# Hybrid MLA and Mamba-2 trunk on one core: flat joint moving operand, SSM scores one step later, gated y transposed through both bank pairs

## Chip, cores and metric

The kernel runs on one core of one Trainium2 chip. The core has a matrix engine (TensorE, PE in the profile; its weight loads are PEld), a vector engine (DVE), a scalar engine (ACT), GpSimd (POOL), and a queue engine (SP) that issues most DMAs. The metric is the device time of one execution in microseconds. The kernel before took 2306.25 us (median of 3 runs, 2304.0 to 2308.58).

## What is computed

The reference is a trunk of two layers over 256 tokens with 2048 channels. Layer 0 mixes tokens with multi-head latent attention (MLA), layer 1 with a Mamba-2 state space block (SSM); each mixer is followed by a dense MLP with squared ReLU and 8192 hidden channels, and everything is pre-norm and residual. Cut to what the change touches:

```python
def ssm_mixer(h, w_in, conv_w, conv_b, dt_bias, a_log, d_skip, norm_g, w_out):
    z, xbc, dt = jnp.split(h @ w_in, ...)
    xbc = silu(causal_depthwise_conv(xbc, conv_w, conv_b))
    xs, b_in, c_in = jnp.split(xbc, ...)        # 8 groups; b_in, c_in have 128 states each
    cb = einsum('blgn,bsgn->blsg', c_c, b_c)    # the scores of a group
    y = einsum('blsgh,bsghp->blghp', cb * decay, x_c) + d_skip * xs
    y = y * silu(z)                             # gated y
    y = rms_norm over each group of 512 channels
    return y @ w_out

def squared_relu_mlp(h, w_in, w_out):
    u = relu(h @ w_in)
    return (u * u) @ w_out
```

The sequence is one chunk of 256, so there is no state carried between chunks.

## The kernel before, in words

**Products in three parts.** Every large product is made from split numbers. A weight tile (128 x 1024 f32, two k tiles of 512 columns) arrives by DMA as `wraw`. ACT copies it rounded into `wh` (line 102), and DVE subtracts to get the rest, `wl` (line 103). Activations are split in the same way. PE then does high times high, low times high and high times low into one PSUM bank. One such piece of weights is called a unit here; in a plain block it is twelve matmuls of 512 columns, eight with `wh` (lines 328 and 329) and then four with `wl` (line 332). There are four `wh` and four `wl` buffers, and the conversions run up to three units ahead.

**Activations as stationary or as moving operand.** The normalised activations lie in four `xt` tiles made by `pair()` (line 278): `[P, 2, 4, 256]`, that is first the high parts of four k tiles and then their low parts. In the plain blocks 128 x 128 pieces of them are the stationary operand. In `column_unit` (line 420) the weights are stationary and the activations move: the matmul of line 425 takes high and low of one k tile together as 2 x 256 moving columns, which lie 1024 elements apart, and that of line 427 takes the high 256 columns alone against `wl`. `column_unit` makes the first columns of each MLP (tiles `cf`) and b and c of the SSM (tiles `acc`).

**Ticks.** The order of PE's instructions is the order in which the program text emits them. Around the blocks, small pieces of work are put off with `self.later(n, fn)`, and `tick()`, called after each key of a block (24 matmuls, two units) and inside `bc_columns`, counts them down: `later(0, ...)` runs at the next tick, `later(2, ...)` at the third. The order on DVE, ACT, POOL and SP is made by a scheduler that sees data dependences and buffers; each engine then runs its list in order.

**SSM.** For each of the 8 groups, `bc_columns(g)` makes b and c, `conv` convolves them (lines 1131 to 1142, result `bc`, one buffer), and `cb_group(g)` makes the scores `cb` on PE (lines 1199 and 1200) into an `sm` bank, which DVE masks (line 1203) and ACT copies (line 1208). `x_block(g)` makes and convolves x and asks for the heads; `head` multiplies decay and scores into `mt` (line 1296), and when eight heads are there `products` runs 64 small matmuls (line 1311) into two `yp` banks, y_0 and y_1. `across` (line 1265) is the far half. `z_block(g)` makes the gate; `gate` multiplies it in, normalises, and `transposes` (line 306) turns the gated y with PE (line 313), after which ACT and DVE split it into k tiles (lines 302 and 303). The order of the steps is the list `SSM_ORDER`: b0, d0, x0, b1, x1, b2, x2, z0, b3, x3, z1, b4, x4, z2, o0 and so on.

**PSUM.** Eight banks: `acc` has four, `sm` two and `yp` two. `bank(wide)` (line 266) gives an `sm` bank when `wide` is False, and takes `yp` and `sm` in turn when it is True. The two transposes of a gated y (one for each half of the tokens) call it with False and take both `sm` banks.

Of the kernel before, what the change touches and what calls it, by code (L numbers as in the profile page):

```python
# [21 lines left out]
F32R = mybir.dt.float32r  # L22
# [6 lines left out]
P = 128  # L29
# [185 lines left out]
class Trunk:  # L215
# [60 lines left out]
        return pool.tile([P, 4, 256], dt, tag=pool.name, name=self.name(pool.name))  # L276

    def pair(self, dt=F32R):
        return self.xtp.tile([P, 2, 4, 256], dt, tag="xt", name=self.name("xt"))

    def rsqrt(self, ssq, n, width, eps=EPS, scale=None):
# [139 lines left out]
    def column_unit(self, acc, unit, xw, half):  # L421

        h, lo = (v.rearrange("p (k n) -> p k n", n=P) for v in unit)
        nc = self.nc
        high = lambda k: nc.tensor.matmul(acc.rearrange("p (i n) -> p i n", i=2), h[:, k], xw[2 * half + k // 4][:, :, k % 4],  # L425
                                          start=half == 0 and k == 0, stop=half == 1 and k == 7)
        low = lambda k: nc.tensor.matmul(acc[:, 0:256], lo[:, k], xw[2 * half + k // 4][:, 0, k % 4], start=False, stop=False)
        for k in range(8):
            for fn in ((low, high) if half and k == 7 else (high, low)):
                fn(k)  # L430
# [636 lines left out]
    def ssm_body(self, sp, dp, gain):  # L1067
        nc, d, cst = self.nc, self.d, self.cst
# [5 lines left out]
        dt = sp.tile([P, 2, 64], F32, name="dt")  # L1074
# [26 lines left out]
        def behind(what):  # L1101
            return self.tc.issue_after(getattr(self.flow, what).ins)
# [14 lines left out]
        def bc_columns(g):  # L1117
            accs = [self.acc_tile() for _ in range(2)]
            for half in range(2):
                for i in range(2):  # L1120
                    self.column_unit(accs[i], self.flow.next(("sb", i, g, half))[1], self.xT, half)
                    if i == 0:
                        self.tick()
            s, a, th = (self.scratch() for _ in range(3))
            of = lambda v: v.rearrange("p (i n) -> p i n", i=2)
            for i in range(2):
                nc.scalar.activation(of(s)[:, i], accs[i][:, 256:512], AF.Copy)
                nc.vector.tensor_tensor(of(s)[:, i], accs[i][:, 0:256], of(s)[:, i], ALU.add)

            def conv():  # L1130
                nc.vector.tensor_tensor(of(s), of(s), row.unsqueeze(1).to_broadcast([P, 2, S]), ALU.mult)
                for i in range(2):
                    c = 8 * i + g
                    wc = lambda k: cst[:, C_CW + 4 * c + k:C_CW + 4 * c + k + 1]
                    u, o = of(s)[:, i], of(a)[:, i]
                    nc.scalar.activation(o, u, AF.Identity, bias=cst[:, C_CB + c:C_CB + c + 1], scale=wc(3))
                    for k in (2, 1, 0):
                        m = 3 - k
                        nc.vector.scalar_tensor_tensor(o[:, m:256], u[:, 0:256 - m], wc(k), o[:, m:256], ALU.mult, ALU.add)
                nc.scalar.activation(th, a, AF.Tanh, scale=0.5)  # L1140
                bc[g] = sp.tile([P, 2, S], F32, tag="bc", name=f"bc{g}", bufs=1)
                nc.vector.scalar_tensor_tensor(bc[g].rearrange("p i n -> p (i n)"), th, 1.0, a, ALU.add, ALU.mult)

            self.later(0, conv)
            self.later(2, lambda: cb_group(g))

        def dt_block():
            self.narrow_block(("si", "dt", 0, 0), self.xT, dt_chain)
# [47 lines left out]
        def cb_group(g):  # L1196
            B, C = bc[g][:, 0], bc[g][:, 1]
            b = self.bank(False)
            nc.tensor.matmul(b[:, 0:256], B[:, 0:P], C, start=True, stop=True)
            nc.tensor.matmul(b[:, 256:384], B[:, P:256], C[:, P:256], start=True, stop=True)  # L1200
            t = sp.tile([P, 384], F32, tag="cb", name=f"cb{g}", bufs=3)
            for o in (0, 256):
                nc.vector.scalar_tensor_tensor(t[:, o:o + P], b[:, o:o + P], 0.125, tri[:, 0:P], ALU.mult, ALU.mult)
            cb[g] = t

            def far_part():
                with behind("last"):
                    nc.scalar.activation(t[:, P:256], b[:, P:256], AF.Copy, scale=0.125)

            self.later(0, far_part)  # L1210
# [111 lines left out]
        yT = [None] * GROUPS  # L1322

        def z_block(g):
            accs = self.block([("si", "z", g, q) for q in range(4)], xT)
            ng = self.gain_tile(d["sng"][g])
            ssq = self.stat(2)
            ws = []
            for t in range(2):
                w = self.scratch()  # L1330
                nc.scalar.activation(w, accs[t], AF.Tanh, scale=rsh[t])
                nc.vector.scalar_tensor_tensor(w, w, 1.0, accs[t], ALU.add, ALU.mult)
                ws.append(w)
            yT[g] = (self.ktile(self.k4), self.ktile(self.k4))

            def gate():
                if g not in ready:
                    self.later(0, gate)
                    return
                for t in range(2):  # L1340
                    x = xg[g][t]
                    nc.gpsimd.tensor_tensor(x, ws[t], x, ALU.mult)
                    self.square_sum(x, ssq[:, t:t + 1], scale=rs[t])
                rr = self.rsqrt(ssq, 2, 512, 4 * EPS)
                r = self.stat(2)
                nc.vector.tensor_tensor(r, rr, rs2, ALU.mult)
                for t in range(2):
                    nc.vector.scalar_tensor_tensor(ws[t], xg[g][t], r[:, t:t + 1], ng, ALU.mult, ALU.mult)
                    self.later(1, lambda t=t: self.transposes(ws[t], yT[g][0], yT[g][1], t, False))
                self.later(1, lambda: gated.add(g))  # L1350

            self.later(1, gate)
# [6 lines left out]
        for step in SSM_ORDER:  # L1359
            kind, i = step[0], int(step[1])  # L1360
            if kind == "b":
                bc_columns(i)
            elif kind == "d":
                dt_block()
            elif kind == "x":
                x_block(i)
            elif kind == "z":
                z_block(i)
            elif i < 3:
                for nb in range(4) if len(step) == 2 else ((0, 1) if step[2] == "a" else (2, 3)):  # L1370
                    self.add_residual(nb, o_block(i, nb))
            else:
                self.boundary_begin(gain)
                for pair in ((0, 1), (2, 3)):
                    accs = {}
                    for nb in pair:
                        accs[nb] = self.block([("so", 6, nb)], self.from_tiles(yT[6:8]), last=False)
                    for nb in pair:
                        self.block([("so", 7, nb)], self.from_tiles(yT[7:8]), accs=accs[nb], first=False)
                        self.finalize(nb, accs[nb], False)  # L1380
                self.boundary_end()
# [228 lines left out]
```

## Time and profile before

| | us |
|---|---|
| median of 3 runs | 2306.25 |
| lowest and highest of them | 2304.0 and 2308.58 |
| the profiled execution, its own time | 2310.83 |
| span of that execution in the profile | 2309.0 |
| PE busy in the span | 2290.7 |
| DVE busy | 1930.3 |
| ACT busy | 1398.8 |
| POOL busy | 208.5 |

Rows of the timeline read: start in us, length in us, engine, line, operation, output and inputs, shape, how many instructions are merged, and in brackets the idle time just before, with what ended it. The ends of matmuls are modelled, since they are pipelined: a single 512-column matmul is shown as 0.39 us, though the next one starts 0.227 us after it. Starts are therefore the safer part of a row. The windows view gives for each stretch the busy time of each engine with its number of instructions, then the granted TensorE clock (1.00 is full speed), the DMA share and GB/s.

### The profile page before, as it was taken

What the parts mean: (1) busy time and instruction counts of PE and PEld (TensorE: products, weight loads), DVE (VectorE), ACT (ScalarE), POOL (GpSimd) and SP (SyncE); (2) the same over time, 40 slices, a digit from 0 to 9 for tenths busy, and PEclk for the clock granted to TensorE, in tenths of its full rate; (3) what the DMA queues carried; (4) which work ended last, traced back from release to release, by engine and by line L of the source; (5) the groups of instructions that cost most, each with busy time, mean ns of one, the idle gap of its engine ahead of it and who ended that gap; (6) DMA issues with size and microseconds to landing.
All of it is one profiled execution on the core that took longest, in us unless ns stands there. A gap on an engine that the chain in (4) does not pass through costs nothing.

```text
span 2309.0 us, 30976 instructions
## 1 busy us (share of the span) xinstructions
PE 2290.7 (99%) x11125; PEld 1908.9 (83%) x11125; DVE 1930.3 (84%) x2379; ACT 1398.8 (61%) x1997; POOL 208.5 (9%) x233
## 2 busy tenths in 40 slices
PE   9999999999999999999999999999999999999999
PEld 8888888888888888888778888888888888888887
DVE  7776798899899897769788678777989889889885
ACT  7775576566666656555555555545666656666663
POOL 1430000000000000002122012120000000000000
PEclk9999999999999999999999999999999999999999
DMA  8444677887887878678777776666688788787874
GB/s 315 147 133 150 206 223 253 260 238 250 262 243 247 268 210 268 196 226 315 259 235 234 248 242 223 223 204 197 201 250 239 251 264 249 239 268 240 250 230 163
DMA packets 161915, 538.02 MB, mean 233 GB/s; under 512 B 17680, under 2 KB 26832, under 8 KB 160736
## 3 DMA queue, kind: packets, MB, share of 16 engines
q1 hardware_dynamic: 151264, 502.36, 65.6%
q0 software_dynamic: 8096, 29.41, 7.8%
q10 hardware_dynamic: 2400, 4.27, 0.5%
q8 instruction: 87, 1.43, 0.3%
q14 instruction: 68, 0.56, 0.1%
HBM read 529.56 MB, written 6.41 MB: 232 GB/s over the span
## 4 chain that ended last, share of the span: by engine, by line
PE 84%; DVE 9%; DMA 3%; issue 2%; POOL 1%; ACT 1%; SPq 0%; DVEq 0%; ACTq 0%; POOLq 0%
PE acc L328 10%; PE acc L329 10%; PE acc L332 10%; PE yp L620 8%; PE yp L621 8%; PE yp L619 8%; PE st L620 7%; PE st L621 7%; PE st L619 7%; DVE wl L103 4%; PE sm L313 2%; PE acc L425 1%; DMA wraw<-mi 1%; DVE xtm L1243 1%; DVE wraw L183 1%
## 5 line engine op out<-in xcount | busy, mean ns | idle before, releaser
L102 ACT ACTIVATE wh<-wraw 128x1024 fp32r<-128x1024 f32 (+1 forms) x818 | 857.4, 1053 | 578.8 <-PE acc L329 247.7
L103 DVE TENSOR_TENSOR wl<-wraw,wh 128x1024 fp32r<-128x1024 f32 (+1 forms) x818 | 983.0, 1216 | 224.1 <-ACT wh L102 213.0
L619 PE MATMUL yp<-wh,k 128*128 128x512 f32 x896 | 350.1, 391 | 0.0
L620 PE MATMUL yp<-wl,k 128*128 128x512 f32 x896 | 349.0, 389 | 0.2 <-DVE wl L103 0.2
L621 PE MATMUL yp<-wh,k 128*128 128x512 f32 x896 | 349.0, 389 | 0.0
L102 ACT ACTIVATE wh<-wrx 128x1024 fp32r<-128x1024 f32 x168 | 177.7, 1059 | 126.2 <-PE yp L621 101.3
L103 DVE TENSOR_TENSOR wl<-wrx,wh 128x1024 fp32r<-128x1024 f32 x168 | 203.9, 1219 | 34.8 <-ACT wh L102 34.6
L328 PE MATMUL acc<-wh,xt 128*128 128x512 f32 x576 | 229.2, 398 | 0.4 <-ACT wh L102 0.4
L329 PE MATMUL acc<-wh,xt 128*128 128x512 f32 x576 | 225.2, 391 | 0.0
L620 PEld LDWEIGHTS yp<-wl,k 128*128 128x128 f32 x896 | 168.2, 188 | 35.4 <-DVE wl L103 0.9
L621 PEld LDWEIGHTS yp<-wh,k 128*128 128x128 f32 x896 | 168.2, 188 | 35.2
L619 PEld LDWEIGHTS yp<-wh,k 128*128 128x128 f32 x896 | 168.2, 188 | 34.7
L328 PE MATMUL acc<-wh,k 128*128 128x512 f32 x496 | 196.5, 396 | 0.0
L329 PE MATMUL acc<-wh,k 128*128 128x512 f32 x496 | 193.2, 390 | 0.0
L619 PE MATMUL st<-wh,xt 128*128 128x512 f32 x448 | 177.2, 396 | 0.0
L620 PE MATMUL st<-wl,xt 128*128 128x512 f32 x448 | 174.8, 390 | 0.0
L621 PE MATMUL st<-wh,xt 128*128 128x512 f32 x448 | 174.8, 390 | 0.0
L332 PE MATMUL acc<-wl,xt 128*128 128x512 f32 x576 | 154.3, 390 | 1.9 <-DVE wl L103 1.9
L199 POOL DMA_DIRECT2D wrx<-mi x56 | 49.1, 877 | 1142.2 <-DVE wl L103 977.1
L332 PE MATMUL acc<-wl,k 128*128 128x512 f32 x496 | 132.9, 390 | 0.7 <-DVE wl L103 0.7
L620 PE MATMUL st<-wl,sN 128*128 128x512 f32 x336 | 131.1, 390 | 1.7 <-DVE wl L103 1.7
L619 PE MATMUL st<-wh,sN 128*128 128x512 f32 x336 | 132.1, 393 | 0.0
(303 smaller groups left out, 3694.4 us busy)
## 6 DMA issues: line engine op xcount, KB each, us to landing
wraw<-mo SPq DMA_DIRECT2D x256, 512.0 KB, 5.3
wraw<-mi SPq DMA_DIRECT2D x224, 512.0 KB, 5.4
wraw<-si SPq DMA_DIRECT2D x128, 512.0 KB, 4.8
wraw<-so SPq DMA_DIRECT2D x64, 512.0 KB, 4.7
wrx<-mi SPq DMA_DIRECT2D x56, 512.0 KB, 4.8
wrx<-mi POOLq DMA_DIRECT2D x56, 512.0 KB, 8.0
wraw<-wo SPq DMA_DIRECT2D x32, 512.0 KB, 3.9
wraw<-mc SPq DMA_DIRECT2D x32, 512.0 KB, 4.4
```

The source lines that it names most:

```text
L102: self.last = nc.scalar.activation(h[:, v], raw[:, v], AF.Copy)
L103: self.last_lo = nc.vector.tensor_tensor(lo[:, v], raw[:, v], h[:, v].bitcast(F32), ALU.subtract)
L183: add = lambda out, a, b: nc.vector.tensor_tensor(st[out].tile, st[a].tile, st[b].tile, ALU.add)
L199: nc.gpsimd.dma_start(st["b11"].tile, quarter(d, 1, 0), accum_op=ALU.add)
L313: self.nc.tensor.transpose(b[:, j * P:(j + 1) * P], src[:, j * P:(j + 1) * P], self.ident)
L328: nc.tensor.matmul(accs[t][:, :n], ah, wh[:, q, :], start=first and kt + q == 0, stop=False)
L329: nc.tensor.matmul(accs[t][:, :n], al, wh[:, q, :], start=False, stop=False)
L332: nc.tensor.matmul(accs[t][:, :n], lhs(kt + q, t)[0], wl[:, q, :], start=False, stop=en and q == nk - 1)
L425: high = lambda k: nc.tensor.matmul(acc.rearrange("p (i n) -> p i n", i=2), h[:, k], xw[2 * half + k // 4][:, :, k % 4], start=half == 0 a ...
L619: nc.tensor.matmul(b, ah, wh, start=first and q == 0, stop=False)
L620: nc.tensor.matmul(b, ah, wl, start=False, stop=False)
L621: nc.tensor.matmul(b, al, wh, start=False, stop=last and q == 1)
```

## The change

Three edits, each of a line or two.

1. `pair()` lays out the split activations as `[P, 4, 2, 256]` in memory, high and low of one k tile side by side, and hands them on under the old index order. The tiles of MLA's attention, which are not split, keep the old layout. In `column_unit` the moving operand of high and low is then one run of 512 elements.
2. `cb_group(g)` runs one tick later, `later(3)` in place of `later(2)`.
3. The transposes of the gated y take the default `wide=True`, so that of the two banks one is a `yp` and one an `sm`.

```diff
     def pair(self, dt=F32R):
+
+        if dt == F32R:
+            return self.xtp.tile([P, 4, 2, 256], dt, tag="xt", name=self.name("xt")).rearrange("p k i n -> p i k n")
         return self.xtp.tile([P, 2, 4, 256], dt, tag="xt", name=self.name("xt"))
...
-        high = lambda k: nc.tensor.matmul(acc.rearrange("p (i n) -> p i n", i=2), h[:, k], xw[2 * half + k // 4][:, :, k % 4],
+        high = lambda k: nc.tensor.matmul(acc, h[:, k], xw[2 * half + k // 4][:, :, k % 4].rearrange("p i n -> p (i n)"),
                                           start=half == 0 and k == 0, stop=half == 1 and k == 7)
...
             self.later(0, conv)
-            self.later(2, lambda: cb_group(g))
+            self.later(3, lambda: cb_group(g))
...
-                    self.later(1, lambda t=t: self.transposes(ws[t], yT[g][0], yT[g][1], t, False))
+                    self.later(1, lambda t=t: self.transposes(ws[t], yT[g][0], yT[g][1], t))
```

Lines behind `pair()` stand three lower in the changed text, so line 1199 is there 1202, 1311 is 1314, 303 is 306 and 1203 is 1206. The number of instructions is the same. What the change does to the order shows in three places. The numbers at the end of a name count buffers.

**PE, the scores of group 3** (tick in x3, with the eight heads of group 1 behind it). `wl_10292` is the last unit before it. Before, the scores and then the products:

```order
L332 MATMUL acc_10226<-wl_10292,xt_8676 128x512
L1199 MATMUL sm_10399<-bc_10279 128x256
L1200 MATMUL sm_10399<-bc_10279 128x128
L1311 MATMUL y_0_10405<-xtm_9470,mt_9924 64x64 x2
L1311 MATMUL y_1_10406<-xtm_9470,mt_9924 64x64 x2
L1311 MATMUL y_0_10405<-xtm_9470,mt_9932 64x64 x2
```

With the change, the transposes two units earlier, then what stands behind the same unit:

```order
L335 MATMUL acc_10226<-wl_10230,xt_8575 128x512
L316 MATMUL yp_10333<-cst,s_700_10082 128x128 x4
L316 MATMUL sm_10340<-cst,s_701_10085 128x128 x4
L331 MATMUL acc_10225<-wh_10247,xt_8676 128x512
L332 MATMUL acc_10225<-wh_10247,xt_8676 128x512
```

```order
L335 MATMUL acc_10226<-wl_10292,xt_8676 128x512
L1314 MATMUL y_0_10399<-xtm_9469,mt_9924 64x64 x2
L1314 MATMUL y_1_10400<-xtm_9469,mt_9924 64x64 x2
L1314 MATMUL y_0_10399<-xtm_9469,mt_9932 64x64 x2
L1314 MATMUL y_1_10400<-xtm_9469,mt_9932 64x64 x2
```

The first transpose writes a `yp` bank now, and the products, which take both `yp` banks, stand where the scores stood; the scores come two units later, directly ahead of line 1265 (1268 in the changed text).

**PE, the scores of group 4** (tick in x4; no products stand here). Before:

```order
L332 MATMUL acc_10857<-wl_10915,xt_8676 128x512
L1199 MATMUL sm_11022<-bc_10910 128x256
L1200 MATMUL sm_11022<-bc_10910 128x128
L328 MATMUL acc_10856<-wh_10932,xt_8777 128x512
L329 MATMUL acc_10856<-wh_10932,xt_8777 128x512
```

With the change:

```order
L335 MATMUL acc_10857<-wl_10989,xt_8777 128x512
L1202 MATMUL sm_11074<-bc_10910 128x256
L1203 MATMUL sm_11074<-bc_10910 128x128
L1268 MATMUL sm_11082<-s_747_10954,cb_10493 128x512
L331 MATMUL acc_11098<-wh_11006,xt_8474 128x512
```

The units with `wl_10933` and `wl_10989` stand ahead of the scores now. The same holds for group 6.

**DVE at the same place.** `k_731` is the low part of the transposed gated y, `bc_10910` the input of the scores. Before:

```order
L103 TENSOR_TENSOR wl_10933<-wraw_10858,wh_10932 128x1024
L1142 TENSOR_SCALAR bc_10910<-s_741_10851,s_740_10850 128x512
L1251 TENSOR_SCALAR xtm_10511<-s_744_10894,xtm_10511 128x512
L1251 TENSOR_SCALAR xtm_10511<-s_745_10949,xtm_10511 128x512
L303 TENSOR_TENSOR k_731_10697<-sm_10956,k_730_10696 128x4x128
L303 TENSOR_TENSOR k_731_10697<-sm_10963,k_730_10696 128x4x128
L1296 TENSOR_SCALAR mt_10980<-mt_10980,dt,cb_10402 128x128 x2
L103 TENSOR_TENSOR wl_10989<-wraw_10876,wh_10988 128x1024
L103 TENSOR_TENSOR wl_11007<-wraw_10912,wh_11006 128x1024
L1203 TENSOR_SCALAR cb_11025<-sm_11022,tri 128x128 x2
```

With the change:

```order
L103 TENSOR_TENSOR wl_10933<-wraw_10858,wh_10932 128x1024
L1145 TENSOR_SCALAR bc_10910<-s_741_10851,s_740_10850 128x512
L1254 TENSOR_SCALAR xtm_10510<-s_744_10894,xtm_10510 128x512
L1254 TENSOR_SCALAR xtm_10510<-s_745_10949,xtm_10510 128x512
L306 TENSOR_TENSOR k_731_10697<-yp_10956,k_730_10696 128x4x128
L306 TENSOR_TENSOR k_731_10697<-sm_10963,k_730_10696 128x4x128
L1299 TENSOR_SCALAR mt_10980<-mt_10980,dt,cb_10493 128x128 x2
L103 TENSOR_TENSOR wl_10989<-wraw_10876,wh_10988 128x1024
L103 TENSOR_TENSOR wl_11007<-wraw_10912,wh_11006 128x1024
L1299 TENSOR_SCALAR mt_11024<-mt_11024,dt,cb_10493 128x128 x2
```

Up to the conversion of `wl_11007` the list is the same. The masking of the scores (line 1203, now 1206) leaves this place and follows three conversions later. Outside the SSM block no engine's list changes its order.

## The prediction

> **What bounds the kernel now.** I read the page first, then the waits of PE, then windows and timelines around the waits found.
>
> ```profile
> span 2309.0 us, 30976 instructions
> PE 2290.7 (99%) x11125; PEld 1908.9 (83%) x11125; DVE 1930.3 (84%) x2379; ACT 1398.8 (61%) x1997; POOL 208.5 (9%) x233
> PE 84%; DVE 9%; DMA 3%; issue 2%; POOL 1%; ACT 1%; SPq 0%; DVEq 0%; ACTq 0%; POOLq 0%
> ```
>
> PE is busy 99% of the span and makes 84% of the chain of waits. So time comes from three places only: idle time of PE, matmuls issued further apart than they need be, and stretches at a lower clock. The waits of PE, with total, number and longest:
>
> ```profile
> PE sm L1199 <- DVE k L303: 5.1, 2, 2.8
> PE acc L332 <- DVE wl L103: 2.6, 4, 1.3
> PE sm L1199 <- DVE bc L1142: 1.6, 1, 1.6
> ```
>
> The largest are three waits of the scores (L1199). Two are for L303, the read-out of a transposed gated y, whose sm bank the scores need; one is for the scores' input bc. They all lie in the SSM block:
>
> ```profile
> 960.00:1560.00 600.00, 590.07 (x3156) 488.45 (x3155) 474.22 (x662) 327.52 (x533) 89.50 (x53) 0.99 0.73 238
> 1121.00:1123.00 2.00, 2.00 (x20) 1.60 (x21) 2.00 (x5) 0.08 (x1) 0.00 (x0) 0.50 0.55 207
> 1188.00:1190.00 2.00, 2.00 (x6) 1.72 (x7) 2.00 (x4) 0.00 (x0) 0.25 (x1) 0.50 0.68 269
> 1190.00:1192.00 2.00, 2.00 (x8) 1.58 (x7) 2.00 (x6) 0.00 (x0) 0.00 (x0) 0.67 0.39 88
> ```
>
> PE idles 9.9 us in this block, and behind two of the waits the clock is halved: 0.50 in two of these windows and 0.67 in the next. The sum is made against the profiled execution's own 2310.83 us, of which its span is 2309.0; that is 4.58 above the median of 2306.25, and I take the difference in us over to the median.
>
> **The change, part by part.** PE around the three waits; I call them A (group 3), B (group 4) and C (group 6).
>
> ```profile
> 1117.06 1.20 PE L332 MATMUL acc<-wl,xt 128*128 128x512 f32 x4 [0.62 <-DVE wl L103]
> 1120.60 1.22 PE L1199 MATMUL sm<-bc 128*128 128x256 f32 x2 [2.35 <-DVE k L303]
> 1122.18 3.68 PE L1311 MATMUL y<-xtm,mt 128*64 128x64 f32 x64
> 1125.79 0.80 PE L328 MATMUL acc<-wh,xt 128*128 128x512 f32 x1
> ...
> 1184.17 1.07 PE L332 MATMUL acc<-wl,xt 128*128 128x512 f32 x4
> 1188.00 1.22 PE L1199 MATMUL sm<-bc 128*128 128x256 f32 x2 [2.76 <-DVE k L303]
> 1189.30 0.77 PE L328 MATMUL acc<-wh,xt 128*128 128x512 f32 x1
> 1192.15 1.07 PE L332 MATMUL acc<-wl,xt 128*128 128x512 f32 x4
> ...
> 1351.90 1.07 PE L332 MATMUL acc<-wl,xt 128*128 128x512 f32 x4
> 1354.60 0.67 PE L1199 MATMUL sm<-bc 128*128 128x256 f32 x2 [1.63 <-DVE bc L1142]
> 1355.24 0.47 PE L328 MATMUL acc<-wh,xt 128*128 128x512 f32 x1
> 1357.17 1.07 PE L332 MATMUL acc<-wl,xt 128*128 128x512 f32 x4
> 1359.89 1.07 PE L332 MATMUL acc<-wl,xt 128*128 128x512 f32 x4
> ```
>
> A unit repeats every 1359.89 - 1357.17 = 2.72 us, so a 512-column matmul takes 2.72 / 12 = 0.227, four of them 0.91 and the eight ahead of the wl part 1.81. By starts, PE could have gone on at 1184.17 + 0.91 = 1185.08 in B and at 1352.81 in C. It waited until 1188.00 and 1354.60: **2.92 us in B, 1.79 in C**.
>
> *The scores a tick later.* In B and C the two units that stood behind the scores come first. What PE then needs is their wl. DVE there:
>
> ```profile
> 1119.87 1.28 DVE L303 TENSOR_TENSOR k<-sm,k 128x512 fp32r<-128x512 f32 x2
> 1121.06 0.60 DVE L1296 SCALAR_TENSOR_TENSOR mt<-mt,dt,cb 128x128 f32<-128x128 f32 x2
> ...
> 1184.32 1.22 DVE L103 TENSOR_TENSOR wl<-wraw,wh 128x1024 fp32r<-128x1024 f32 x1
> 1185.45 0.69 DVE L1142 SCALAR_TENSOR_TENSOR bc<-s,s 128x512 f32<-128x512 f32 x1
> 1187.26 1.28 DVE L303 TENSOR_TENSOR k<-sm,k 128x512 fp32r<-128x512 f32 x2
> 1188.98 2.36 DVE L103 TENSOR_TENSOR wl<-wraw,wh 128x1024 fp32r<-128x1024 f32 x2
> 1199.79 1.23 DVE L103 TENSOR_TENSOR wl<-wraw,wh 128x1024 fp32r<-128x1024 f32 x1 [0.18 <-ACT wh L102]
> ...
> 1350.44 1.22 DVE L103 TENSOR_TENSOR wl<-wraw,wh 128x1024 fp32r<-128x1024 f32 x1
> 1353.77 0.68 DVE L1142 SCALAR_TENSOR_TENSOR bc<-s,s 128x512 f32<-128x512 f32 x1
> 1354.97 2.35 DVE L103 TENSOR_TENSOR wl<-wraw,wh 128x1024 fp32r<-128x1024 f32 x2
> ```
>
> B: the first unit starts at 1185.08 and needs its wl at 1185.08 + 1.81 = 1186.89; that conversion (1184.32, 1.22) ends at 1185.54, in time. The second starts at 1187.80 and needs its own at 1189.61; it is the first of the pair at 1188.98 and ends at 1190.20, so PE waits **0.59**. The scores come at about 1191.1, with bc done at 1186.14 and both sm banks free from 1188.54. C: the wl of the first unit is done at 1351.66, that of the second at about 1356.2 and needed at 1352.81 + 2.72 + 1.81 = 1357.34. No wait there. What would be late next is DVE: it stands still for the first time after B at 1199.6, waiting for ACT and ACT for PE, so by then it has caught up with PE.
>
> With the wait of B the halved clock behind it goes too. From 1188.00 to 1192.15, scores and eight matmuls took 4.15; the same pieces in C, at full clock, took 1357.17 - 1354.60 = 2.57. That is **1.58**, and I count it whole: the new wait of 0.59 is as short as the 0.62 in the row of 1117.06.
> B gives 2.92 + 1.58 - 0.59 = 3.91, C 1.79.
>
> The page TensorE: Matmul & The Clock Gate of the Trainium skill (section HAM oscillation — how this bites in real kernels) says that only idle gaps of more than about 3.4 us bring the clock down. Here 2.92 us of idle time were enough, with 0.50 granted in the window behind them, so the trace differs. By the rule the clock would not be bought back with the wait, and my sum would be 1.58 smaller.
>
> *The gated y through both bank pairs.* This alone frees an sm bank for the scores, but at A the products take the place of the scores, and they need both yp banks, one of which now holds the first transposed half. Its read-out is the first of the two L303 at 1119.87, ending at 1120.5, the very instruction for which the scores waited until 1120.60. DVE's list is unchanged up to it. So at A the wait only moves from L1199 to the first matmul of y_1, and the half clock stays as well. Its bounds: 0 if L303 stays where it is, and if it came early enough the whole wait, 1120.60 - 1117.06 - 0.11 - 0.91 = 2.52 (0.11 for the first wl matmul, still slow), plus the halved clock behind it, for which the 1.58 of B is the nearest number, together 4.1. I take 0, since no row of DVE moves. Behind the wait POOL starts on y some 1.2 us earlier (the scores no longer stand ahead of it), which DVE's next stall inherits; PE has two converted units in hand there, so I count nothing. Elsewhere the products come at least 70 matmuls (16 us) behind a transpose, so the yp bank is free.
>
> *The flat operand.*
>
> ```profile
> 271.80 1.07 PE L332 MATMUL acc<-wl,k 128*128 128x512 f32 x4
> 272.70 0.39 PE L425 MATMUL cf<-xt,wh 128*128 128x512 f32 x1
> 275.16 0.40 PE L425 MATMUL cf<-xt,wh 128*128 128x512 f32 x1
> 28.76 3.83 PE sm L347 x32
> L425 PE MATMUL acc<-xt,wh 128*128 128x512 f32 x256 | 91.2, 400 | 0.0
> L425 PE MATMUL cf<-xt,wh 128*128 128x512 f32 x256 | 90.8, 398 | 0.0
> ```
>
> Seven pairs of high and low take 275.16 - 272.70 = 2.46, or 351 ns each. Flat operands of the same widths elsewhere: 227 for 512 columns, and 3.83 / 32 = 120 for 256 columns (L347, a narrow block with its own flat operand), together 347. There are 512 pairs. Bounds: 0, if the 4 ns come from the alternation of widths and not from the gap in the operand, and 512 x 4.4 ns = 2.2 us. I take the middle, 1.1, less a fifth, because the 96 pairs of groups 1 to 3 lie ahead of A, where DVE sets the time whatever PE gained: **0.9**. Nothing excludes a loss, but no flat operand in these rows is slower than this one. The writers (L302, L303) keep their runs of 128 elements at a wider step; that costs them nothing I can see, and they are not what PE waits for outside A.
>
> The page SBUF — State Buffer of the Trainium skill (section Specifications (TRN2)) puts the price of a read at each crossing to a new 16-byte line. Two runs of 256 floats cross as many lines as one of 512, so by this rule the edit gives 0 and the sum is 0.9 smaller; the rows leave 0 to 2.2.
>
> Sum: 3.91 + 1.79 + 0 + 0.9 = 6.6 us. 2310.83 - 6.6 = 2304.2 for the profiled execution; on the median **2306.25 - 6.6 = 2299.7 us**.
>
> **Rivals.** 0.2% of 2306.25 is 4.6 us, about what a measurement of this kernel tells from no change: faster is below 2301.6, slower above 2310.9.
>
> 1. *The wait goes over to wl.* DVE is full from 1184 to 1199, so PE, let through at B, may pay the 2.92 back in waits at L332. Then B gives only the clock, 1.58, C nothing, the flat operand 0.9: 2306.25 - 2.5 = 2303.8, no change. For it: DVE is just in time at A already (0.62 on wl). Against it: the two conversions that B needs are early or 0.59 late, and C's are early.
> 2. *The waits do not go at all.* The scores find another dependence, or the later scores hold up line 1265 right behind them: 2306.25 - 0.9 = 2305.3. Against it: bc and both banks are free 2.5 us before the scores.
> 3. *A goes too.* If L303 reads out the yp bank soon after the transposes, another 4.1 come off: 2295.6. Against it: the unchanged list of DVE.
> 4. *Slower.* DVE works in order, and line 1203 waits for the scores, which come two units (5.44 us) later. Where DVE reaches it first, the conversions behind it stand still. It decides from the point at which DVE would idle there for longer than the two converted units that PE has in hand; PE would then lack two conversions, 2.36 us (row of 1188.98), at each of 8 groups: 18.9 - 6.6 = 12.3 slower, 2318.5. Against it: line 1203 moves behind three conversions or more in DVE's list as well, at B from 1191 to about 1198.
>
> **How the numbers follow.** Forecast 0.56, rival 1 0.22, rival 2 0.07, rival 3 0.10, rival 4 0.05. Faster: 0.56 + 0.10 = 0.66; within 0.2%: 0.22 + 0.07 = 0.29; slower 0.05. The likeliest case alone spans 2297.5 to 2301.9 (flat operand 0 or 2.2, clock of B kept, give or take the 2 us by which single runs differ from the median). The range reaches down to rival 3 and up over rivals 1 and 2: 2295.5 to 2305.5. It leaves out rival 4 and the far sides of 2 and 3.
>
> **What would show it.** Right: no wait at L1199 any more (line 1202 there); PE waits some 2.6 us at L1311 (1314), y_1, once, for L303 (306), with the clock at 0.50 behind it; the window that answers to B at 1.00; a wait on wl of about 0.6 there; pairs of L425 at 347 ns. Wrong: waits at L332 for wl that grow by as much as L1199 loses (rival 1); DVE idle in front of line 1203 (rival 4); pairs still at 351 (0.9 less); no wait of the products (rival 3).

## The result, and the profile after

The changed kernel takes 2301.72 us (median of 14 runs), the kernel before in the same comparison 2307.69 (14 runs, 2304.0 to 2310.99). Of the changed kernel's runs, one took 2521.44 us at a mean granted clock of 0.851 and is left out of the ratio; the other thirteen lie between 2300.03 and 2303.49, with a median of 2301.48. The ratio is 0.9974, 95% interval 0.9966 to 0.9982: 6.0 us faster (6.2 by the thirteen). Predicted were 2299.7, 6.6 less than the 2306.25 that the kernel before had then.

The head of the page of the changed kernel, and the waits of PE in its trace (total us, times, longest):

```profile
span 2300.3 us, 30967 instructions
PE 2287.0 (99%) x11125; PEld 1906.6 (83%) x11125; DVE 1930.0 (84%) x2379; ACT 1401.6 (61%) x1997; POOL 210.5 (9%) x233
```

```profile
PE acc L335 <- DVE wl L103: 2.2, 5, 0.6
PE y L1314 <- DVE k L306: 2.1, 1, 2.1
```

The span is 8.7 us shorter than the profiled one of before. The waits of the scores, 5.1 and 1.6, are gone, and one wait of the products has come. The same stretch as before in windows (span of the window; busy time of PE, PEld, DVE, ACT and POOL; granted clock; DMA share; GB/s), with two windows at A and one at B:

```profile
960.00:1560.00 600.00, 595.74 (x3196) 493.62 (x3195) 479.41 (x670) 334.07 (x541) 95.24 (x56) 1.00 0.73 241
1116.63:1120.04 3.41, 1.33 (x46) 1.24 (x44) 3.41 (x8) 1.44 (x4) 1.27 (x1) 1.00 0.87 282
1120.04:1123.45 3.41, 3.41 (x31) 2.87 (x27) 2.62 (x4) 2.90 (x11) 2.31 (x1) 0.50 0.50 145
1182.00:1192.00 10.00, 9.51 (x41) 7.24 (x41) 10.00 (x19) 5.87 (x8) 1.34 (x1) 1.00 0.74 260
```

PE idles 4.3 us in the block (9.9 before), B runs at full clock, and at A one window of 3.41 us is halved (it was two before). PE at the three places, from the timeline of the changed kernel:

```profile
1115.26 1.20 PE L335 MATMUL acc<-wl,xt 128*128 128x512 f32 x4 [0.60 <-DVE wl L103]
1116.38 0.34 PE L1314 MATMUL y<-xtm,mt 128*64 128x64 f32 x4
1118.80 2.47 PE L1314 MATMUL y<-xtm,mt 128*64 128x64 f32 x60 [2.08 <-DVE k L306]
...
1128.47 1.02 PE L1268 MATMUL sm<-s,cb 128*128 128x512 f32 x2
...
1186.14 0.39 PE L332 MATMUL acc<-wh,xt 128*128 128x512 f32 x1
1187.02 1.20 PE L335 MATMUL acc<-wl,xt 128*128 128x512 f32 x4 [0.49 <-DVE wl L103]
1188.06 0.59 PE L1202 MATMUL sm<-bc 128*128 128x256 f32 x2
...
1350.29 1.07 PE L335 MATMUL acc<-wl,xt 128*128 128x512 f32 x4
1351.19 0.59 PE L1202 MATMUL sm<-bc 128*128 128x256 f32 x2
```

A: the first four products are issued, and the others wait for L306, the read-out of the `yp` bank. B: the scores no longer wait; the wait ahead of them is for wl, 1187.02 - 1186.14 - 0.227 = 0.65. C: the scores follow their unit after 0.90, the pitch of four matmuls, so there is no wait.

Before, the same stretch of work at A ended here:

```profile
1131.68 1.02 PE L1265 MATMUL sm<-s,cb 128*128 128x512 f32 x2
```

Four terms make the difference of the two profiles. B gives 2.92 + 1.58 - 0.65 = 3.85. C gives 1.79. At A the same work (wl part, products, scores, two units, line 1268) took 1128.47 - 1115.26 = 13.21; before, it ran from the wl part at 1117.06 to line 1265 at 1131.68, 14.62, so A gives 1.41. Together that is 7.05. The other 1.6 are two shorter waits for wl ahead of A (0.74 to 0 at 1032, 1.45 to 0.55 at 1105). The second of them is 1.39 again in another profile of edits 2 and 3 (below), so I do not put them down to the change.

### The profile page after: what moved, and what is told of

Same layout as the page of the kernel before. It is cut to its first block, busy times and chain, and to the rows that moved or that the text cites. A ratio compares the mean times of both kernels' runs of the same rounds, so it can differ in the third digit from the quotient of the medians.

```text
span 2300.3 us, 30967 instructions
## 1 busy us (share of the span) xinstructions
PE 2287.0 (99%) x11125; PEld 1906.6 (83%) x11125; DVE 1930.0 (84%) x2379; ACT 1401.6 (61%) x1997; POOL 210.5 (9%) x233
```

## The experiments

### Each edit alone, and edits 2 and 3 without the flat operand

Four kernels on one chip, with the kernel before at 2308.34.

**Edit 1 alone**: lines 278 and 425 as in the change, the rest as before.

> The kernel before with the flat joint operand alone. Theory 1 (the gap in the moving operand costs nothing, since pairs of high and low take 351 ns in the changed kernel too): ratio 1.000, within 0.05% of before, pairs still 351 ns, all three waits of the scores still there. Rival (the prediction's term): pairs at 347 ns and 0.9 us less, ratio 0.9996; 2.2 us less (0.9990) at most.

Measured: 2308.10 (11 runs), ratio 1.0001 [0.9993, 1.001]. Its waits of PE are those of before (line numbers two higher):

```profile
PE sm L1201 <- DVE k L305: 5.1, 2, 2.8
PE acc L334 <- DVE wl L103: 2.6, 4, 1.3
PE sm L1201 <- DVE bc L1144: 1.6, 1, 1.6
```

The time alone does not exclude the rival's 0.9 us, for its ratio of 0.9996 lies in the interval; the pairs do. Over 426 pairs of high and low, from one high matmul to the next, the mean is 351.4 ns before, 351.6 in this kernel and 351.2 in the changed one (gaps over 380 ns left out). In the timeline of the changed kernel, six pairs take 275.80 - 273.69 = 2.11, 352 each:

```profile
273.69 0.39 PE L428 MATMUL cf<-xt,wh 128*128 128x512 f32 x1
273.91 0.28 PE L430 MATMUL cf<-xt,wl 128*128 128x256 f32 x1
...
275.80 0.40 PE L428 MATMUL cf<-xt,wh 128*128 128x512 f32 x1
```

So the 4 ns over 227 + 120 do not come from the gap in the operand. That they belong to the alternation of widths is what is left, and no run tests it. The edit is worth nothing that these runs can see.

**Edit 2 alone**:

```diff
-            self.later(2, lambda: cb_group(g))
+            self.later(3, lambda: cb_group(g))
```

> The kernel before with the scores a tick later alone; the gated y stays in the two sm banks. Theory 1 (the wait at A in the changed kernel is the products' own wait for the yp bank that the gated y took): no wait at the scores in A, B and C and none at the products, clock at full speed throughout the SSM block; the changed kernel's 6.0 us and another 2.2 us of wait and 1.7 us of halved clock, 9 to 10 us less than before, ratio 0.9958, about 4 us less than the changed kernel. Rival (the scores still wait for an sm bank, or DVE cannot feed PE any sooner at A and the wait turns into waits for wl): not faster than the changed kernel, ratio 0.9974 or more.

Measured: 2299.88 (5 runs, 2299.24 to 2300.26), ratio 0.9968 [0.9956, 0.9981]: 8.5 us less than before, short of the 9 to 10 expected, and better than the whole change. There is no wait at the scores or the products, and no halved clock before the last matmuls. What is left at A, from PE's timeline:

```profile
1114.75 1.19 PE L332 MATMUL acc<-wl,xt 128*128 128x512 f32 x4 [0.62 <-DVE wl L103]
1115.87 2.09 PE L1311 MATMUL y<-xtm,mt 128*64 128x64 f32 x64
...
1124.06 1.21 PE L332 MATMUL acc<-wl,xt 128*128 128x512 f32 x4 [1.34 <-DVE wl L103]
1125.11 0.59 PE L1199 MATMUL sm<-bc 128*128 128x256 f32 x2
1125.76 1.02 PE L1265 MATMUL sm<-s,cb 128*128 128x512 f32 x2
```

The products go through at once, since both `yp` banks are free, and the work that took 14.62 before and 13.21 in the change takes 1125.76 - 1114.75 = 11.01. A new wait of 1.34 for wl stands there; its cause comes below.

**Edit 3 alone**:

```diff
-                    self.later(1, lambda t=t: self.transposes(ws[t], yT[g][0], yT[g][1], t, False))
+                    self.later(1, lambda t=t: self.transposes(ws[t], yT[g][0], yT[g][1], t))
```

> The kernel before with the gated y through both bank pairs alone; the scores stay at their old tick. Theory 1: at A the scores go through at once and the products wait some 2 us for the read-out of the yp bank instead; at B the scores wait for bc alone, about 1.1 us in place of 2.9, with no halved clock behind it; at C the wait of 1.8 us for bc stays. 3 to 4 us less than before, ratio 0.9985. Rival (the sm bank was not what held the scores up): no change, 1.000.

Measured: 2302.47 (11 runs), ratio 0.9979 [0.997, 0.9988], 5.9 less and so more than I expected. Its waits of PE:

```profile
PE sm L1199 <- DVE bc L1142: 2.6, 2, 1.6
PE y L1311 <- DVE k L303: 1.4, 1, 1.4
```

At A the wait moves to the products and is shorter (1.4 for 2.35, since the scores are issued ahead of it). At B the scores wait only for bc, 0.97 in their row of the timeline, in place of 2.76. The clock is halved at neither; the prediction had it stay halved at A. At C the wait for bc is still there (1.6, the longest in its row), as expected.

**Edits 2 and 3**, the change without edit 1:

> The changed kernel without the flat operand: scores a tick later and the gated y through both bank pairs. Theory 1 (the flat operand is worth nothing): equal to the changed kernel, ratio 0.9974, with the same wait of about 2.1 us at the products in A. Rival: 0.9 to 2.2 us slower than the changed kernel, ratio 0.9978 to 0.9984.

Measured: 2302.18 (11 runs), ratio 0.9979 [0.997, 0.9988]. This interval holds both the 0.9974 of the whole change and the rival's 0.9978 to 0.9984, so the time does not decide between them; by the pairs above, the flat operand adds nothing. The wait of 2.1 us at the products is there. Edit 3 on top of edit 2 costs some 2 us: the slowest run of edit 2 alone took 2300.26, the fastest of edits 2 and 3 took 2300.83.

### The change without edit 3, and without it at one group

Four kernels on a second chip, with the kernel before at 2307.39. The first is the change itself.

> The changed kernel itself, beside the next ones on the same chip. Both theories: ratio 0.9974, with the wait at the products in A (about 2.1 us) and a halved clock of one or two stretches of 3.4 us behind it in most executions.

Measured: 2301.77 (8 runs, 2298.93 to 2302.4), ratio 0.9976 [0.9966, 0.9986]. Its profiled execution is its fastest, and the wait at A, 2.06 us in it, brought no halved clock; that is taken up in the last section.

**Edits 1 and 2** (edit 3 left out):

> The changed kernel without its third edit: flat operand and later scores, gated y in the two sm banks. Theory 1 (the third edit puts a wait of its own at A): no wait at the products, 1.5 us of wait for wl there instead, no halved clock, equal to the later scores alone, 2299.9 us, ratio 0.9965, 2 us less than the changed kernel. Rival (the third edit does nothing once the scores are late, and the low median of five runs was luck): equal to the changed kernel, 0.9974.

Measured: 2300.25 (5 runs, 2298.92 to 2300.49), ratio 0.9968 [0.9956, 0.9981]. PE does not wait at the products, its longest wait for wl is 1.3 us, and the clock is not halved before the last matmuls. So it is edit 2 alone again, as expected.

**The change, with only the gated y of group 0 back in the `sm` banks**:

```diff
-                    self.later(1, lambda t=t: self.transposes(ws[t], yT[g][0], yT[g][1], t))
+                    self.later(1, lambda t=t: self.transposes(ws[t], yT[g][0], yT[g][1], t, g > 0))
```

> The changed kernel, except that the gated y of group 0, the one ahead of A, stays in the two sm banks; the other seven groups use both pairs. Theory 1 (the whole price of the third edit is at A): equal to later_flat, 2299.9 us, 0.9965. Rival (it costs a little at each group): no more than a quarter of a microsecond less than the changed kernel.

Measured: 2299.48 (6 runs, 2298.82 to 2300.38), ratio 0.9968 [0.9956, 0.998], which is 2.3 below the change on the same chip and no higher than with edit 3 left out everywhere. One pair of transposes is all that differs, the pair whose bank the products at A wait for. So the whole price of edit 3 lies at A.

**Edits 1 and 2, with the read-out of the gated y's low parts a tick later and behind the last conversion**, so that the wl at A comes earlier:

```diff
+        def low():
+            with self.tc.issue_after(self.flow.last_lo.ins) if behind else nullcontext():
+                self.nc.vector.tensor_tensor(lo, b, h.bitcast(F32), ALU.subtract)
...
+        if behind:
+            self.later(0, low)
```

> later_flat, and DVE's read-out of the low part of the gated y is put off by a tick and behind the last conversion issued, so that two conversions come ahead of it at A. Theory 1 (at A DVE is the bound: whatever comes first, the rest is late): the 1.5 us of wait for wl at A go, and the scores wait for the sm bank about as long, since the read-out now stands behind the accumulation of y, which waits for POOL; equal to later_flat within 1 us. Rival (PE waits for the order of DVE's list, not for its work): 1 to 1.5 us less than later_flat, about 2298.6.

Measured: 2306.82 (11 runs), ratio 0.9998 [0.9989, 1.0007]. Both expectations missed; nearly the whole gain is given back. Its waits of PE, then DVE at A (the read-out is line 321 here, the scores 1211):

```profile
PE sm L1211 <- DVE k L321: 3.9, 2, 3.3
PE acc L341 <- DVE k L321: 1.8, 1, 1.8
```

```profile
1117.36 2.44 DVE L1308 SCALAR_TENSOR_TENSOR mt<-mt,dt,cb 128x128 f32<-128x128 f32 x2
1119.72 4.54 DVE L103 TENSOR_TENSOR wl<-wraw,wh 128x1024 fp32r<-128x1024 f32 x2
...
1125.90 1.28 DVE L321 TENSOR_TENSOR k<-sm,k 128x512 fp32r<-128x512 f32 x2
```

The late read-out holds the `sm` banks, so the scores wait again, now 3.3 us, with the halved clock behind it. The second row is a wait near the end of the block, at 1511, for the same read-out, with one more halved window behind it. The rows hold a hint as well: two conversions take 4.54 there in place of 2.36, and two mt 2.44 in place of 0.60. Something slows DVE at A.

### What slows DVE at A

In edit 2 alone, DVE and then POOL at A:

```profile
1118.76 4.11 DVE L1296 SCALAR_TENSOR_TENSOR mt<-mt,dt,cb 128x128 f32<-128x128 f32 x4
1122.79 2.35 DVE L103 TENSOR_TENSOR wl<-wraw,wh 128x1024 fp32r<-128x1024 f32 x2
...
1126.26 1.13 DVE L1296 SCALAR_TENSOR_TENSOR mt<-mt,dt,cb 128x128 f32<-128x128 f32 x4
```

```profile
1117.27 1.27 POOL L1261 TENSOR_TENSOR s<-xtm,edge 128x512 f32<-128x512 f32 x1 [16.66 <-PE y L1311]
1118.51 2.58 POOL L1314 TENSOR_TENSOR xtm<-xtm,gb 128x512 f32<-128x512 f32 x2
1121.17 1.29 POOL L1316 TENSOR_TENSOR xtm<-xtm,far 128x512 f32<-128x512 f32 x1
```

Four mt take 4.11 us beside POOL's last three instructions, and 1.13 once POOL is idle. Taken singly in the trace, the first three take 1.19, 1.37 and 1.44 us, and each ends 0.15 us behind the end of one of POOL's; the fourth takes 0.34. POOL ends at 1122.46, and the next conversion starts at 1122.79. The page SBUF — State Buffer of the Trainium skill (section SBUF: two separate sides) says that a DVE instruction with two SBUF inputs and a GpSimd instruction that reads SBUF exclude each other for the whole instruction; the rows agree. To try it, POOL's instructions on the products of group 1 (in the rows, lines 1314 and 1316) were made to need the second conversion behind them (`low` in the diff), by adding its difference with itself, which is zero, to an operand:

```diff
+                if g == 1:
+                    low = self.flow.low[:, 0:2].bitcast(F32)
+                    zero = self.stat(2)
+                    nc.gpsimd.tensor_tensor(zero, low, low, ALU.subtract)
+                    nc.gpsimd.tensor_tensor(dg[:, 0:2], dg[:, 0:2], zero, ALU.add)
                 for t in range(2):
                     x = xg[g][t]
                     nc.gpsimd.tensor_tensor(x, x, dg, ALU.mult)
```

Three kernels on a third chip, with the kernel before at 2308.94. First edits 1 and 2 as they were:

> The scores a tick later with the flat operand, once more, as the reference on this chip for the two kernels beside it. About 2300.2 us, 0.9968 of the kernel before; at A (group 3) one wait of 1.3 us for wl, while four instructions of mt (L1298) on DVE take 4.1 us instead of 1.1.

Measured: 2299.51 (5 runs, 2298.16 to 2299.84), ratio 0.9958 [0.9946, 0.9971].

> The kernel beside it, but POOL's three instructions on y_1 (L1322, L1324), which start behind the products of group 1, are made to wait for the second conversion behind them. Theory that POOL's instructions hold up those of DVE that run beside them: the four mt at A take 1.1 us again, the pair of conversions ends 3 us earlier, the wait of 1.3 us for wl goes, and the kernel is 1.3 to 1.5 us faster than the one beside it, about 2298.8. Rival, that DVE is late there for another reason (its list, DMA): mt stays at 4.1, the wait stays, no difference. Second rival, that POOL's instructions hold up the next two conversions in place of mt: the wait comes one or two units later, no difference in time.

Measured: 2297.68 (5 runs, 2297.05 to 2299.55), ratio 0.9953 [0.994, 0.9967], 1.8 below the kernel beside it. The runs of the two overlap (2297.05 to 2299.55 and 2298.16 to 2299.84), so the trace has to say where it came from. PE, DVE and POOL at A:

```profile
1114.41 1.19 PE L335 MATMUL acc<-wl,xt 128*128 128x512 f32 x4 [0.62 <-DVE wl L104]
...
1122.21 1.07 PE L335 MATMUL acc<-wl,xt 128*128 128x512 f32 x4
...
1123.77 1.02 PE L1268 MATMUL sm<-s,cb 128*128 128x512 f32 x2
```

```profile
1118.42 1.13 DVE L1299 SCALAR_TENSOR_TENSOR mt<-mt,dt,cb 128x128 f32<-128x128 f32 x4
1119.46 2.35 DVE L104 TENSOR_TENSOR wl<-wraw,wh 128x1024 fp32r<-128x1024 f32 x2
1121.74 2.18 DVE L1299 SCALAR_TENSOR_TENSOR mt<-mt,dt,cb 128x128 f32<-128x128 f32 x4
```

```profile
1122.49 2.57 POOL L1322 TENSOR_TENSOR xtm<-xtm,gb 128x512 f32<-128x512 f32 x2
```

The four mt are back at 1.13, the conversions follow at once, and PE does not wait: the work takes 1123.77 - 1114.41 = 9.36 where it took 11.01. The price is paid behind it, by the next mt (2.18), for which nobody waits. So POOL's instructions were the cause of the wait at A. The spans of the two profiles differ by 0.5 us only (2296.4 and 2295.9): ahead of A, where the edit changes nothing, a wait for wl at 1104 was 0.7 longer in this execution, and 0.5 was lost again far behind the block (2183 to 2202).

> The same wait at all eight groups. Theory: only at A is DVE what PE waits for, so nothing more is gained than with group 1 alone: about 2298.8. Rival: the instructions that POOL holds up elsewhere cost time too, then up to 1 us less; or the later y comes too late for its gate at some group, then more than the kernel with group 1 alone.

Measured: 2298.90 (5 runs, 2297.48 to 2299.55), ratio 0.9956 [0.9943, 0.9968]. The wait at A is gone here too, and the other groups give nothing more, as expected; two waits for wl, at 1232 and 1395, are 0.3 longer than in edits 1 and 2. The lowest median of the study is that of edits 1 and 2 without edit 3, with the wait at group 1 alone; its runs overlap with those of the two kernels beside it.

## Why the prediction was right, and where it was not

**B** was right, step by step: no wait at the scores, the clock at 1.00, a new wait for wl of 0.65 (0.59 predicted), 3.85 in all (3.91). **C** was right: 1.79 gone, no wait for wl. Rivals 1 and 2 do not hold: in place of 2.92 and 1.79 there is one new wait for wl, the 0.65 at B, and the scores wait for nothing. Rival 4 does not hold: PE waits for nothing that line 1206 (1203 before) holds up.

**A** was right about the mechanism. The wait moved from the scores to the first products, for the same read-out, and by about the predicted size (2.08 in the row, some 2.6 predicted). Mis-sized was the term "the half clock stays as well": it stayed for one window of 3.41 us where before it had two, and in the second profile of the change for none. So A gave 1.41 us in the profiled execution, not 0.

**The flat operand** was the step that failed: 0.9 predicted, nothing measured. The lower of its two bounds, 0, was the true one: the price of 4.4 ns was put on the gap in the operand without a run that had tried it, and without the gap the pairs take the same 351. The page SBUF — State Buffer of the Trainium skill (section Specifications (TRN2)), by whose rule the edit gives 0, fits the runs.

**What the sum hid.** B, C, A and the flat operand were 3.91 + 1.79 + 0 + 0.9 and came out as 3.85 + 1.79 + 1.41 + 0, or 7.05 in place of 6.6: two errors of about 1 us partly cancel. That the medians, 6.0 apart, are also near 6.6 is partly luck, for the clock's share of the sum was read from one execution and is not the same in every run (last section). The prediction costed edit 3 at A at 0, as a wait that only moves. Against edit 2 alone it is a loss: with both `yp` banks free the products need not wait at all. That was there to be seen: before, the gated y took `sm` banks only, so the products, which take `yp` banks, did not depend on its read-out. Also, "I count nothing" for POOL's earlier start was right in the change, where POOL starts after the conversions have begun (line 1317 at 1121.14), but with edit 2 alone that start costs 1.65 us.

## What to carry to other kernels

A wait for a bank is not removed by taking the bank from another pool if the instructions that then come first need that pool: ask of each pool who needs it next. When a change moves one engine's work earlier, look at what runs beside it on the others, for at the same place in DVE's list the four mt take 4.1 us beside POOL's instructions and 1.1 without them. Try each edit of a bundle alone; here one of three gained 8.5 us alone, one nothing, and one, which gained 5.9 alone, took back 2.3 beside the first.

## What the runs showed of the clock

The halved clock lies on a fixed grid. In the profile of before the clock stands at full for 1112.745 us, at half for 6.827, at full for 61.440, at half for 3.413: 326, 2, 18 and 1 times 3.413 us. In the changed kernel it is 1112.745 at full and 3.413 at half. Laid on that grid, the profile of before reads (columns as above; PE's busy time is the first after the comma):

```profile
1116.23:1119.64 3.41, 1.40 (x5) 0.67 (x4) 3.41 (x5) 2.77 (x4) 0.07 (x1) 1.00 0.97 367
1119.64:1123.05 3.41, 2.45 (x20) 2.05 (x22) 3.41 (x7) 0.13 (x1) 1.21 (x1) 0.50 0.69 228
...
1184.49:1187.90 3.41, 0.75 (x4) 0.28 (x2) 3.41 (x6) 3.04 (x4) 0.99 (x1) 1.00 0.96 372
1187.90:1191.31 3.41, 3.31 (x9) 2.74 (x10) 3.41 (x7) 0.00 (x0) 0.35 (x1) 0.50 0.48 180
1351.70:1355.10 3.40, 1.77 (x8) 1.22 (x7) 3.40 (x7) 2.10 (x3) 1.04 (x1) 1.00 0.95 351
1355.10:1358.50 3.40, 3.40 (x17) 2.85 (x16) 3.40 (x5) 1.13 (x2) 0.00 (x0) 1.00 0.66 213
```

The second profile of the change, where the same wait at A fell across two windows:

```profile
1112.50:1115.91 3.41, 1.91 (x10) 0.88 (x9) 3.41 (x5) 3.01 (x4) 0.00 (x0) 1.00 0.91 368
1115.91:1119.32 3.41, 2.22 (x61) 2.13 (x62) 3.41 (x7) 1.84 (x7) 1.55 (x2) 1.00 0.73 265
1119.32:1122.74 3.42, 3.42 (x16) 2.79 (x15) 3.42 (x3) 2.97 (x9) 3.34 (x3) 1.00 0.64 191
```

Windows with PE busy for 0.75, 1.33 (the changed kernel at A, above) and 1.40 us are followed by a halved one, and windows with 1.77, 1.91 and 2.22 are not. The same wait of 2.1 us therefore halves the clock or does not, by where it falls on the grid. The kernel with the late read-out brings the two sides closer, at its wait of 1.8 us:

```profile
1509.30:1512.71 3.41, 1.58 (x7) 0.81 (x6) 3.00 (x3) 1.23 (x4) 3.02 (x2) 1.00 0.50 144
1512.71:1516.12 3.41, 3.41 (x9) 2.64 (x9) 2.11 (x4) 2.46 (x4) 0.70 (x1) 0.50 0.41 142
```

With the grid laid over all thirteen traces in the same way, every window at full clock in which PE was busy for 1.58 us or less is followed by a halved one (eleven of them, three at the very end of a run), and none with 1.66 or more is; the 1.66 is that of edit 1 alone at 2303.32. So in these traces the point lies between 1.58 and 1.66 us of 3.413, by the profile's modelled busy time, and the length of the idle time alone does not decide. The halved window with 2.45 was followed by a second one, that with 3.31 was not; what it takes to come back is not settled by these rows.

The page TensorE: Matmul & The Clock Gate of the Trainium skill (section Part 1: The HAM clock gate) tells of a free-running window of 3413 ns, which these runs show. The rule that the prediction took from the same page, that only gaps of more than about 3.4 us bring the clock down, they contradict.

The scatter of single runs goes with this. Among the 27 runs of the kernel before in the first set of experiments, the six with a mean granted clock of 1.000 took 2303.86 to 2305.85 us, the ten with 0.998 took 2308.01 to 2310.95. It is not the whole scatter: the eleven runs of edit 3 alone all have 1.000 and lie between 2300.66 and 2304.13. The profiled execution that the prediction was worked on, 2310.83, was one of the long ones, and part of what it promised is not there to be gained in every run: 8.7 us between the two profiles, 6.0 between the medians.
